# Expert weights in ten 16 KB places with 2 MB transfers, a front section laid out for them, and a filled router stretch

## The chip, the cores and the metric

The kernel runs on one core of a Trainium2 chip, as a single program. The metric is the device time of one execution in microseconds (us); lower is better. Before the change the median of three runs is 1062.04 us (1060.44 to 1062.28).

A core has a matrix engine (TensorE, PE in the profile, with its weight loads shown apart as PEld), a vector engine (VectorE, DVE), an activation engine (ScalarE, ACT), GpSimd (POOL) and a small engine that here only issues transfers (SyncE, SP). Sixteen DMA engines move data between the main memory and the on-chip memory SBUF, which has 128 partitions. TensorE accumulates in PSUM banks of 512 floats per partition. TensorE's clock has two levels, 1.2 and 2.4 GHz; the profile shows the granted one as a share of the full speed.

## The reference, cut to what matters

One encoder layer on 256 tokens of width 1024, in float32: token mixing by three mixers side by side, a LayerNorm, and then a mixture of 32 experts, of which each token uses 4, and a second LayerNorm.

```
z = x @ w_in + b_in                                   # 1024 -> 2304
y_pool = pool_mixer(z[0:256])                         # 4 centred means, a small linear map, a scale
y_attn = neighbourhood_attention(q, k, v, rpb)        # 8 heads of 64, tokens on a 4 x 64 grid, 16 columns wide
y_conv = conv_module(a, gate)                         # GLU, 31 taps, LayerNorm, swish, 256 x 256
x = layer_norm(ALPHA * x + concat(y_pool, y_attn, y_conv) @ w_out + b_out)
logits = x @ w_router + b_router
gates = softmax over the 4 largest logits, 0 elsewhere
for e in range(32):
    g = min(x @ w_gate[e] + b_gate[e], 7);  u = clip(x @ w_up[e] + b_up[e], -7, 7)
    out += gates[:, e] * (((u + 1) * g * sigmoid(1.702 * g)) @ w_down[e] + b_down[e])
x = layer_norm(ALPHA * x + out)
```

Each expert has three matrices of 1024 x 1024 floats, 12 MiB; all 32 are 384 MiB and have to pass through SBUF once. Everything else that is read is below 20 MiB.

## The kernel before

The program is written in order, engine by engine; nothing reorders it. It has two halves.

**The front.** The input projection is done in five column groups (`W_IN_GROUPS`): convolution, q, k, pooling, v. For q, k and v each raw weight is split into a high and a low part (`split`, lines 105 to 108: ACT makes the high part, DVE the rest), and three fast products stand for one exact one (`zstep`). Scores, softmax, the products with the values, the pooling and the 31 convolution taps (on DVE, in portions `TAPS`) follow, then the output projection `outproj`, whose weights come as four raw tiles of 1 MB (`wo_raw`). Three of them are split as well; the one in `WHOLE` is used as it is, by a full float32 product. Then come LayerNorm (`stats1`, `apply1`), the transposed activations `hT` (`turn1`), the router's scores, the choice of the four experts per token (`chosen`), and the slot of each token at its expert (`positions`). I call the time from the router's scores to the first expert product the router stretch: PE, DVE and ACT hand small results to each other there.

**The experts.** Each expert takes up to 64 tokens, gathered by a product with a 0/1 matrix (`gather`, line 729, out of `x1n`, which is `xa`). The products with the gate, up and down matrices are lines 761, 761 and 814 (`first`, `down`), each preceded by a product that puts the bias in (line 755). One matmul keeps 64 tokens as its stationary operand and streams 512 weight columns. The results are added to the four PSUM banks `acc` by line 826. The expert with the most tokens is put at number 20 (`FULL`) and gets a second, smaller block there.

**Weights.** SBUF holds twenty places of 8 KB per partition, 1 MiB each over 128 partitions (`slot`, line 89). A weight matrix comes as four transfers of 1 MiB, one per place (`load_rows`, line 136; the transfer itself is line 141), with a row of 8 KB for each partition. The places are taken in the order `places` (line 317) again and again. During the front many of these places hold the front's own tiles, and a weight transfer into such a place has to wait until the front is done with it. `load_ahead` issues expert 0's twelve transfers at three points of the front, and `load_expert` issues those of one further expert each time. All of them go out through SP, in program order: a transfer that waits for its place holds up everything behind it. Besides the place, each transfer waits until the eighth transfer before it has landed, since eight completion semaphores are used in turn.

**What sets the order around the change.** On SP it is the order of the calls; what a transfer waits for is the last reader of its place. On PE the router stretch runs: scores of tokens 128 to 255 (line 611), slots (635, 634, 635), the gather for expert 0 (729), the count of tokens per expert (1007), the bias of expert 0's gate (755) and its gate product (761).

The functions that the diff touches, as they were:

Of the kernel before, what the change touches and what calls it, by code (L numbers as in the profile page):

```python
# [25 lines left out]
CAP2 = 32  # L26
FULL = 20
# [19 lines left out]
def shape_consts():  # L47
# [3 lines left out]
    m = np.full((128, 2, 4, 31), -1e30, np.float32)  # L51
    for q in range(128):
        c2, i = q // 64, 15 - q % 16
        for pair in range(2):
            cb = 2 * pair + c2
            sc = min(max(cb * 16 + i - 8, 0), 48)
            for j in range(31):
                if sc <= BC[cb] + j < sc + 16:
                    m[q, pair, :, j] = 0.0
# [15 lines left out]
def encoder_layer(ctx, tc, xT_d, x_d, w_in, par_d, rows_d, rpb, w_out, cst_d,  # L75
# [14 lines left out]

    def bank(tag="bk"):
# [18 lines left out]
    def load_in(c0, n, places, h0=0):  # L110
# [3 lines left out]
        for h, place in enumerate(places, h0):  # L114
            t = slot(place, f"wi{place}")[:].rearrange("p (k c) -> p k c", c=n)
            nc.sync.dma_start(t, w_in_at[c0][:, h * per:(h + 1) * per, :])
            v.append(t)
        return v

    def halves(places, n):  # L120
        return [slot(p, f"wp{p}", F32R)[:].rearrange("p (k c) -> p k c", c=n) for p in places]

    class Parts:
# [5 lines left out]
        def add(self, raw, places, eng=nc.vector):  # L129
            self.v.append(halves(places, 2048 // self.per))  # L130
            split(raw, *self.v[-1], eng)
# [14 lines left out]
    xT = slot(0, "xT")[:].rearrange("p (k t) -> p k t", k=8)  # L146
    wi_conv = [slot(p, f"wi{p}")[:].rearrange("p (k c) -> p k c", c=512) for p in (1, 2)]
# [4 lines left out]
    wi_q = load_in(256, 512, (3, 4))  # L152
    nc.sync.dma_start(par[:], par_d)
    wi_k = load_in(768, 512, (13, 19))
    wi_p = load_in(0, 256, (14,))

    biasT = slot(17, "biasT")[:].rearrange("p (a h k) -> p a h k", a=2, h=8)
# [20 lines left out]
    wi_v = load_in(1280, 512, (1, 2))  # L178
# [39 lines left out]
    xh, xl = [slot(p, f"x{p}", F32R)[:].rearrange("p (k t) -> p k t", k=8) for p in (15, 16)]  # L218
# [38 lines left out]
    wp_q.add(wi_q[0], (9, 10))  # L257
    wp_q.add(wi_q[1], (11, 12))
    qbs = [bank("bg" if j == 3 else "bk") for j in range(4)]
    zproj(wp_q, qbs)  # L260
    wp_k.add(wi_k[0], (5, 6))
# [5 lines left out]
    wp_k.add(wi_k[1], (7, 8))  # L267
# [21 lines left out]
    wp_v.add(wi_v[0], (9, 10))  # L289
    wp_v.add(wi_v[1], (11, 12))  # L290
    run_taps(TAPS[5])
    add_mask(1)
    qk = slot(18, "qk")[:].rearrange("p (a c t) -> p a c t", a=2, c=4)
    qT, kT = qk[:, 0], qk[:, 1]
    for j in range(4):
        nc.scalar.activation(qT[:, j, :].rearrange("p (b r i) -> p r b i", b=4, r=4),
                             qbs[j][:, :256].rearrange("p (r b i) -> p r b i", r=4, b=4)[:, :, :, ::-1], AF.Identity,
                             bias=bias_in(2 + j), scale=1.0)
    zproj(wp_k, bks)
    for j in range(4):  # L300
        nc.scalar.activation(kT[:, j, :], bks[j][:, :256], AF.Identity, bias=bias_in(6 + j), scale=1.0)
    bias_parts()
    wo_raw = {k: load_rows(p, w_out, k) for k, p in ((1, 21), (0, 3), (2, 4), (3, 13))}
    xa = slot(19, "xa")[:].rearrange("p (t d) -> p t d", t=2)
    nc.sync.dma_start(xa, x_d.rearrange("p (t d) -> p t d", t=2))
    WHOLE = (0,)
    wo_places = ((5, 6), (7, 8), (1, 2), (9, 10))
    wo = {}

    def split_out(k):  # L310

        hi, lo = [slot(p, f"wo{p}", F32R)[:].rearrange("p (k c) -> p k c", k=2) for p in wo_places[k]]
        wo[k] = hi, lo
        assert k not in WHOLE
        split(wo_raw[k], hi, lo)
# [4 lines left out]
    chunks = ((m, k) for m in range(3) for k in ((0, 1, 2, 3), (0, 1, 2, 3), (0, 2, 1, 3))[m])  # L320
# [7 lines left out]

    act_table(AF.Exp)
# [5 lines left out]
    load_ahead(2)  # L335
# [895 lines left out]
```

## Time and profile before

| what | value |
|---|---|
| median of 3 runs | 1062.04 us (1060.44 to 1062.28) |
| profiled execution, its own time | 1060.73 us |
| its span, first to last instruction | 1058.9 us |
| granted TensorE clock, mean | 0.981 |
| PE busy | 986.5 us (93%) |
| DVE, ACT, POOL busy | 307.0, 161.7, 16.3 us |
| bytes moved by DMA | 423.38 MB, mean 400 GB/s |

The span is what the trace covers; the 1.8 us between it and the execution's own time lie around the program. PE's busy share is no measure of how near PE is to its peak. What counts is which wait ends last in each stretch, so the span has to be read in stretches: the front up to about 120 us, the experts after it, and the last 15 us, in which the last bytes have landed and the second LayerNorm and the stores follow. A DMA share near 1.00 means that all sixteen engines always have work.

### The profile page before, as it was taken

Reading aid. Unit: us, or ns where it says so; the run is one execution under the profiler, and the core shown is the slowest. Engines: PE = TensorE matmul, PEld = TensorE weight load, DVE = VectorE, ACT = ScalarE, POOL = GpSimd, SP = SyncE. Lnnn points to the kernel's source line nnn. Section 1 sums busy time; section 2 is a strip of 40 time slices with the busy share of each in tenths; the row PEclk is TensorE's granted clock in tenths of the full one; section 3 lists DMA queues with packets and bytes.
Section 4 is the critical chain, followed back from the end, with each engine's and each line's share of the span. In section 5 each row is a group of like instructions: output and inputs, shape, how many; then the busy total and the mean of one; then the engine's idle time right before and its main releaser. Section 6 shows DMA issues by size and latency. Waiting matters only on the chain.

```text
span 1058.9 us, 13693 instructions
## 1 busy us (share of the span) xinstructions
PE 986.5 (93%) x5202; PEld 431.9 (41%) x5202; DVE 307.0 (29%) x791; ACT 161.7 (15%) x339; POOL 16.3 (2%) x28
## 2 busy tenths in 40 slices
PE   7999999999999999999999898989999998998995
PEld 6977644343434343434333232333434332323232
DVE  4798442222212321212222112221222222112114
ACT  4374211011111011110101010110111110101001
POOL 0110000000000000000000000000000000000001
PEclk9999799999999899999999999999999999999998
DMA  9957799999999999999999999999999999999994
GB/s 373 402 213 318 274 377 421 421 422 421 420 421 421 420 421 421 421 421 421 421 422 418 422 421 421 420 423 419 421 421 422 420 421 421 422 421 420 421 397 169
DMA packets 61710, 423.38 MB, mean 400 GB/s; under 512 B 6886, under 2 KB 7398, under 8 KB 11594
## 3 DMA queue, kind: packets, MB, share of 16 engines
q1 hardware_dynamic: 61114, 421.82, 96.7%
q8 instruction: 42, 0.69, 0.3%
q0 software_dynamic: 384, 0.39, 0.1%
q10 hardware_dynamic: 144, 0.26, 0.1%
q14 instruction: 26, 0.21, 0.1%
HBM read 421.01 MB, written 1.05 MB: 399 GB/s over the span
## 4 chain that ended last, share of the span: by engine, by line
DMA 51%; PE 42%; DVE 3%; ACT 2%; issue 1%; SPq 0%; DVEq 0%; ACTq 0%
DMA w<-in_w_up_dram 18%; DMA w<-in_w_down_dram 16%; DMA w<-in_w_gate_dram 13%; PE bk L761 11%; PE bk L814 10%; PE bg L761 9%; PE bk L729 4%; PE acc L436 2%; DMA cst<-in_cst_dram 2%; DMA wi<-in_w_in_dram 2%; PE acc L826 1%; PE bk L791 1%; DVE cacc L277 1%; ACT sb L358 1%; PE bk L708 1%
## 5 line engine op out<-in xcount | busy, mean ns | idle before, releaser
L761 PE MATMUL bk<-w,xgp 128*64 128x512 f32 x1024 | 239.7, 605 | 13.1 <-DMA w<-in_w_up_dram 13.1
L761 PE MATMUL bg<-w,xgp 128*64 128x512 f32 x1024 | 233.8, 603 | 11.2 <-DMA w<-in_w_gate_dram 11.1
L814 PE MATMUL bk<-w,aT 128*64 128x512 f32 (+1 forms) x1024 | 227.0, 600 | 1.5 <-DMA w<-in_w_down_dram 1.5
L761 PEld LDWEIGHTS bg<-w,xgp 128*64 128x64 f32 x1024 | 72.5, 139 | 161.7 <-issue 118.9
L761 PEld LDWEIGHTS bk<-w,xgp 128*64 128x64 f32 x1024 | 69.1, 138 | 151.6 <-issue 108.3
L814 PEld LDWEIGHTS bk<-w,aT 128*64 128x64 f32 (+1 forms) x1024 | 69.7, 137 | 136.2 <-issue 127.5
L819 DVE SCALAR_TENSOR_TENSOR y<-bk,gs,y 128x512 fp32r<-128x512 f32 x31 | 23.3, 751 | 270.1 <-ACT y L818 270.1
L770 DVE TENSOR_SCALAR g<-bg 128x512 f32<-128x512 f32 x32 | 22.1, 692 | 172.8 <-PE bg L761 172.8
L729 PE MATMUL bk<-se,xa 128*128 128x128 f32 (+1 forms) x544 | 66.8, 284 | 0.5 <-DVE se L720 0.5
L729 PEld LDWEIGHTS bk<-se,xa 128*128 128x128 f32 x544 | 65.3, 200 | 0.6 <-issue 0.6
L793 ACT COPY aT<-bk 128x256 f32<-128x256 f32 (+1 forms) x66 | 24.3, 369 | 240.7 <-PE bk L791 236.2
L771 ACT ACTIVATE s<-g 128x512 f32<-128x512 f32 (+1 forms) x33 | 20.6, 625 | 250.7 <-DVE g L770 250.7
L781 DVE TENSOR_SCALAR u<-bk 128x256 f32<-128x256 f32 (+1 forms) x66 | 27.5, 417 | 93.6 <-PE bk L761 93.6
L818 ACT ACTIVATE y<-bk,gs 128x512 fp32r<-128x512 f32 x31 | 21.3, 687 | 215.2 <-PE bk L814 215.2
L826 PE MATMUL acc<-y,st 64*128 64x512 f32 x248 | 46.3, 447 | 1.1 <-ACT y L818 0.8
L791 PE MATMUL bk<-ident,g 128*128 128x128 f32 x128 | 27.6, 298 | 13.6 <-DVE g L782 12.4
L577 DVE TENSOR_SCALAR xgp<-bk,g1b 128x128 f32<-128x128 f32 (+1 forms) x68 | 22.7, 397 | 51.6 <-PE bk L729 51.6
L575 ACT ACTIVATE xgp<-bk,g1b 128x128 f32<-128x128 f32 (+1 forms) x68 | 25.1, 450 | 82.0 <-PE bk L729 82.0
L711 DVE TENSOR_SCALAR st<-bk 128x256 fp32r<-128x256 f32 x32 | 13.6, 425 | 82.3 <-PE bk L708 82.3
L826 PEld LDWEIGHTS acc<-y,st 64*128 64x128 f32 x248 | 19.1, 186 | 32.0 <-issue 29.5
L772 DVE TENSOR_TENSOR g<-g,s 128x512 f32<-128x512 f32 (+1 forms) x33 | 22.6, 684 | 24.6 <-ACT s L771 24.6
L791 PEld LDWEIGHTS bk<-ident,g 128*128 128x128 f32 x128 | 13.3, 143 | 37.5 <-issue 22.4
(289 smaller groups left out, 666.3 us busy)
## 6 DMA issues: line engine op xcount, KB each, us to landing
w<-in_w_gate_dram SPq DMA_DIRECT2D x127, 1024.0 KB, 19.8
w<-in_w_up_dram SPq DMA_DIRECT2D x127, 1024.0 KB, 19.8
w<-in_w_down_dram SPq DMA_DIRECT2D x124, 1024.0 KB, 19.8
wi<-in_w_in_dram SPq DMA_DIRECT2D x8, 1024.0 KB, 9.8
w<-in_w_out_dram SPq DMA_DIRECT2D x4, 1024.0 KB, 9.3
w<-in_w_down_dram SPq DMA_DIRECT2D x7, 512.0 KB, 8.7
wi<-in_w_in_dram SPq DMA_DIRECT2D x2, 512.0 KB, 6.9
biasT<-in_rpb_dram SPq DMA_DIRECT2D x2, 512.0 KB, 17.5
```

The source lines that it names most:

```text
L575: nc.scalar.activation(o, i, AF.Identity, bias=b, scale=g)
L577: eng.tensor_scalar(o, i, g, b, op0=mult, op1=add)
L729: nc.tensor.matmul(p[:, i * n:(i + 1) * n], x1n[:, tt, (g + i) * 128:(g + i) * 128 + 128], se[:, tt, :], start=(tt == 0), stop=(tt == 1))
L761: nc.tensor.matmul(p[i * c:(i + 1) * c, :n], xg[:, k, :], w[k // 2][:, k % 2, i * n:(i + 1) * n], start=False, stop=(k == 7))
L770: nc.vector.tensor_scalar(g[:], p[:, :n], 7.0, None, op0=ALU.min)
L772: nc.vector.tensor_tensor(g[:], g[:], s[:], op=mult)
L781: nc.vector.tensor_scalar(u[:, o], p[:, o], -7.0, 7.0, op0=ALU.max, op1=ALU.min)
L791: nc.tensor.transpose(p[:, j * 128:j * 128 + 128], a[:, j * 128:j * 128 + 128], ident[:])
L793: nc.scalar.copy(aT[:, o], p[:, :h * 256].rearrange("p (j n) -> p j n", n=128)[:, o])
L814: nc.tensor.matmul(p[o:o + c, :], aT[:, k % h, k // h * c:(k // h + 1) * c], rows_of(w, k, dh), start=(k == of_part[0]), stop=(k == of_par ...
L819: nc.vector.scalar_tensor_tensor(y[:, 1], p[:], gs[:], y[:, 0].bitcast(F32), op0=mult, op1=sub)
L826: nc.tensor.matmul(acc[tt][dh][:], st[dh * 64:dh * 64 + 64, tt, :], y[dh * 64:dh * 64 + 64, i, :], start=(start and i == 0), stop=False, s ...
```

## The change

1. **Places and transfers.** The twenty places of 8 KB become ten of 16 KB (`both`). An expert matrix comes as two transfers of 2 MiB, with a row of 16 KB per partition; `by_chunks` lays the arrays out for that on the host. The rows of the down matrix are stored in the order in which `down` uses them (`DOWN`).
2. **Front.** The front's tiles are put into halves of the new places, in other neighbourhoods, with two places of 8 KB beside them (19 and 20). Expert 0's transfers are issued at four points of the front, and the tile `xa` and the raw output weights 0 and 3 are loaded later.
3. **Expert 1's down matrix** is loaded back into the tiles of expert 0's gate matrix, in five pieces, so that a piece can start as soon as the rows that it overwrites have been used.
4. **Keys and values by grid column.** `kT` and the new `vT` are written with the four tokens of a grid column side by side, so that the 31 columns that a block needs are 124 neighbouring floats. The sixteen copies for `vB` become four. The rpb bands and the mask are laid out to match.
5. **Output projection.** Raw tile 3 is used whole, like tile 0; its split and the low parts for rows 6 and 7 go.
6. **Router stretch.** The sums of the router weights are reduced on DVE first (`gsum`), and one matmul of 64 columns takes the place of eight. Behind the first slots, PE gets the bias product of expert 0's gate (`p0`) and a product of `hT` with the identity into an `acc` bank, which nothing reads. The count of tokens per expert moves ahead of the gather. The gather for expert 1 moves from the middle of expert 0's up product to its transposes, in two halves.

Where the transfers stand on SP: this is the piece of SP's queue before from the raw output weights (`in_w_out_dram`) to the first load of the table `whose`, which tells which expert comes when; a row is one kind of transfer with its count.

```order
L141 DMA w<-in_w_out_dram 128x2048 x4
L305 DMA xa<-in_x_dram 128x2048
L141 DMA w<-in_w_gate_dram 128x2048 x4
L141 DMA w<-in_w_up_dram 128x2048 x4
L141 DMA w<-in_w_down_dram 128x2048 x4
L141 DMA w<-in_w_gate_dram 128x2048 x4
L141 DMA w<-in_w_up_dram 128x2048 x4
L141 DMA w<-in_w_down_dram 128x2048 x4
L928 TENSOR_LOAD whose
```

And the same piece of SP's queue now; `xT`, `wo` and `bias` are the tiles whose halves hold raw output weights.

```order
L143 DMA xT<-in_w_out_dram 128x2048
L143 DMA wo_439<-in_w_out_dram 128x2048
L150 DMA w<-in_w_gate_dram 128x4096 x2
L150 DMA w<-in_w_up_dram 128x4096
L143 DMA wo_447<-in_w_out_dram 128x2048
L150 DMA w<-in_w_up_dram 128x4096
L143 DMA bias<-in_w_out_dram 128x2048
L150 DMA w<-in_w_down_dram 128x4096 x2
L515 DMA xa<-in_x_dram 128x2048
L150 DMA w<-in_w_gate_dram 128x4096 x2
L150 DMA w<-in_w_up_dram 128x4096 x2
L150 DMA w<-in_w_down_dram 128x1024 x2
```

Six weight transfers of 2 MiB now stand between and ahead of the last raw output weights and `xa`; expert 1's down matrix starts with two pieces of 0.5 MiB (three of 1 MiB follow), where it was four transfers of 1 MiB.

PE's queue in the router stretch before, from the second half of the router's scores to the gate product of expert 0 (`bk` and `bg` are PSUM banks, `msk` the chosen experts, `se` the 0/1 matrix of the gather):

```order
L611 MATMUL bk<-gw,hT 128x32 x8
L635 MATMUL bk<-msk,cst 128x32
L634 MATMUL bk<-msk,onesm 128x32
L635 MATMUL bk<-msk,cst 128x32
L729 MATMUL bk<-se,xa 128x64 x16
L1007 MATMUL bk<-msk,onesm 128x32 x2
L755 LDWEIGHTS bsel
L755 MATMUL bg<-bg_101,bsel 64x512
L761 MATMUL bg<-w,xgp 64x512 x16
```

The same stretch of PE's queue now:

```order
L631 MATMUL bk<-gw,hT 128x32 x8
L655 MATMUL bk<-msk,cst 128x32
L678 LDWEIGHTS bsel
L678 MATMUL bg<-bg_98,bsel 64x512
L704 MATMUL acc_72<-hT,ident 128x512
L654 MATMUL bk<-msk,onesm 128x32
L655 MATMUL bk<-msk,cst 128x32
L671 MATMUL bk<-msk,onesm 128x32 x2
L767 MATMUL bk<-se,xa 128x64 x16
L806 MATMUL bg<-w,xgp 64x512 x16
```

The bias and the identity product stand between the first and the second slots, the count stands ahead of the gather, and the gate product follows the gather directly.

The core of the diff:

```diff
+    def both(i, name, dtype=F32):
+        t = slots.tile([128, 4096], dtype, name=name, tag=f"p{i}")[:]
+        return t, (t[:, :2048], t[:, 2048:])
...
-    def load_rows(place, src, k, n=1):
-        t = slot(place, "w")[:]
-        for i in range(n):
-            o = slice(i * 2048 // n, (i + 1) * 2048 // n)
-            nc.sync.dma_start(t[:, o], src[k][:, o])
-        return t.rearrange("p (k c) -> p k c", k=2)
+    def load_rows(place, src, k, cuts=(0, 4), t=None):
+        t = both(place, "w")[0] if t is None else t
+        for a, b in zip(cuts, cuts[1:]):
+            nc.sync.dma_start(t[:, a * 1024:b * 1024], src[k][:, a * 1024:b * 1024])
+        return t.rearrange("p (k c) -> p k c", k=4)
...
-    wo_raw = {k: load_rows(p, w_out, k) for k, p in ((1, 21), (0, 3), (2, 4), (3, 13))}
-    WHOLE = (0,)
-    wo_places = ((5, 6), (7, 8), (1, 2), (9, 10))
+    wo_raw = {1: load_out(wo1, 1), 2: load_out(both(6, "wo2")[1][0], 2)}
+    WHOLE = (0, 3)
+    wo_places = {1: 8, 2: 5}
...
-    places = (5, 6, 0, 15, 16, 21, 4, 11, 12, 3, 13, 7, 8, 1, 2, 18, 14, 9, 10, 17)
+    places = (0, 1, 2, 3, 7, 4, 8, 5, 6, 9)
...
+    load_ahead(3)
+    wo_raw[0] = load_out(slot(19, "wo0")[:], 0)
...
-    vB = slot(17, "vB")[:, :1984].rearrange("p (j b k) -> p j b k", j=4, b=4)
+    vT = b_v[:, :1024].rearrange("p (j t) -> p j t", j=4)
...
-    b = bank()
-    for k in range(8):
-        nc.tensor.matmul(b[:, :64], onesm[:], gw[:, k], start=(k == 0), stop=(k == 7))
+    nc.vector.tensor_reduce(gsum[:], gw[:].rearrange("p k e -> p e k"), axis=AX.X, op=add)
...
+    b = bank()
+    nc.tensor.matmul(b[:, :64], onesm[:], gsum[:], start=True, stop=True)
...
     positions(0)
+    p0 = bank("bg")
+    bias_first(p0, bsel[:, 0:1], 0)
+    nc.tensor.matmul(acc[0][0][:], ident[:], hT[:, 0:2, :], start=True, stop=True)
     chosen(1, i1)
     positions(1)
+    call = keep.tile([128, E], F32, name="call")
+    counts()
...
-        p = first(sel, 0, xg, W[0], tag="bg")
+        p = first(sel, 0, xg, W[0], tag="bg", p=p0 if e == 0 else None)
+        if e == 0:
+            first_tiles = [W[0][k].rearrange("p k c -> p (k c)") for k in range(2)]
+            Wn[2] = {k: load_rows(next(turns), w_down[1], k, ((0, 1, 2, 4), (0, 2, 4))[k], first_tiles[k])
+                     for k in range(2)}
...
-def by_chunks(w):
-    return w.reshape(*w.shape[:-2], 4, 2, 128, 1024).swapaxes(-3, -2).reshape(*w.shape[:-2], 4, 128, 2048)
+def by_chunks(w, n=2, order=range(8)):
+    w = w.reshape(*w.shape[:-2], 8, 128, 1024)[..., list(order), :, :]
+    return w.reshape(*w.shape[:-3], n, 8 // n, 128, 1024).swapaxes(-3, -2).reshape(*w.shape[:-3], n, 128, 8192 // n)
```

## Rows read from the trace of the kernel before

**Rows 1.** The page, bandwidth in 40 equal slices of the span.
```profile
GB/s 373 402 213 318 274 377 421 421 422 421 420 421 421 420 421 421 421 421 421 421 422 418 422 421 421 420 423 419 421 421 422 420 421 421 422 421 420 421 397 169
```

**Rows 2.** The page, the chain of work that ended last, by engine.
```profile
DMA 51%; PE 42%; DVE 3%; ACT 2%; issue 1%; SPq 0%; DVEq 0%; ACTq 0%
```

**Rows 3.** Stretches: stretch and length, busy per engine, PEclk, DMA share, GB/s.
```profile
40.00:120.00 80.00, 75.48 (x546) 64.13 (x545) 65.51 (x141) 41.33 (x102) 9.32 (x17) 0.96 0.78 305
120.00:130.00 10.00, 10.00 (x37) 4.26 (x39) 5.39 (x33) 2.13 (x4) 0.00 (x0) 0.63 0.35 118
130.00:160.00 30.00, 28.55 (x154) 12.06 (x152) 13.48 (x62) 3.35 (x8) 0.00 (x0) 1.00 0.97 380
160.00:1020.00 860.00, 812.41 (x4138) 309.74 (x4136) 189.60 (x501) 94.92 (x205) 0.00 (x0) 0.99 1.01 421
```

**Rows 4.** Timeline of PE: starts of three experts, and the first waits for weights.
```profile
518.04 0.39 PE L755 MATMUL bg<-bg,bselp 96*64 96x512 bf16 x2
542.27 0.39 PE L755 MATMUL bg<-bg,bselp 96*64 96x512 bf16 x2
570.08 0.39 PE L755 MATMUL bg<-bg,bselp 96*64 96x512 bf16 x2
593.01 1.94 PE L814 MATMUL bk<-w,aT 128*64 128x512 f32 x8 [0.25 <-DMA w<-in_w_down_dram]
```

**Rows 5.** What SP waited for: total us, times, longest us.
```profile
SPq L141 <- PE bg L761: 32.2, 22, 14.2
```

**Rows 6.** Timeline of SP's transfer issues: start us, us, then what.
```profile
106.58 4.99 SPq L141 DMA_DIRECT2D w<-in_w_up_dram  x4
125.89 6.36 SPq L141 DMA_DIRECT2D w<-in_w_down_dram  x4
```

**Rows 7.** Timeline of PE, router stretch and first experts: start us, us, then what.
```profile
113.06 0.41 PE L635 MATMUL bk<-msk,cst 128*128 128x32 f32 x2 [1.44 <-DVE msk L628]
114.00 7.06 PE L729 MATMUL bk<-se,xa 128*128 128x64 f32 x32 [0.54 <-DVE se L720]
120.86 1.01 PE L1007 MATMUL bk<-msk,onesm 128*128 128x32 f32 x4
122.22 9.65 PE L761 MATMUL bg<-w,xgp 128*64 128x512 f32 x32
...
135.74 3.68 PE L729 MATMUL bk<-se,xa 128*128 128x64 f32 x32
...
152.62 7.04 PE L761 MATMUL bg<-w,xgp 128*64 128x512 f32 x32
```

**Rows 8.** The page: a transfer queue (packets, MB, share), issues (KB, us to landing).
```profile
q8 instruction: 42, 0.69, 0.3%
...
w<-in_w_gate_dram SPq DMA_DIRECT2D x127, 1024.0 KB, 19.8
...
w<-in_w_down_dram SPq DMA_DIRECT2D x7, 512.0 KB, 8.7
```

**Rows 9.** A stretch in which the last expert's 512 KB transfers land.
```profile
1038.00:1040.00 2.00, 2.00 (x12) 0.72 (x10) 0.00 (x0) 0.06 (x1) 0.00 (x0) 1.00 1.05 387
```

**Rows 10.** Timeline of PE, output projection and the sums for the router.
```profile
73.85 3.70 PE L436 MATMUL acc<-w,more 128*128 128x512 f32 x8 [2.16 <-ACT more L411]
...
79.49 3.70 PE L436 MATMUL acc<-w,more 128*128 128x512 f32 x8
...
90.41 5.85 PE L436 MATMUL acc<-wo,mix 128*128 128x512 f32 x24
96.09 1.90 PE L529 MATMUL bk<-gw,onesm 128*128 128x64 f32 x16
...
99.48 4.62 PE L436 MATMUL acc<-wo,mix 128*128 128x512 f32 x18
...
104.73 1.62 PE L436 MATMUL acc<-wo,mix 128*128 128x512 f32 x6
```

**Rows 11.** Timeline of DVE: the first use of the tile xa.
```profile
94.44 2.49 DVE L522 SCALAR_TENSOR_TENSOR xa<-xa,small 128x512 f32<-128x512 f32 x4
```

More of the change, by code (lines that the diff above doesn't have):

```diff
@@ L26 @@
 CAP2 = 32
+DOWN = (0, 1, 4, 5, 2, 3, 6, 7)
 FULL = 20
@@ L127, in __init__, with add @@
             self.per, self.v = 2048 // n, []
-        def add(self, raw, places, eng=nc.vector):
-            self.v.append(halves(places, 2048 // self.per))
+        def add(self, raw, place, eng=nc.vector):
+            self.v.append(halves(place, "wp", 2048 // self.per))
             split(raw, *self.v[-1], eng)
@@ L382, in encoder_layer @@
             zstep(bks[j], wp_v, k, j)
[L384 to L389 removed]
+    load_ahead(1)
+    wo_raw[3] = load_out(k_wo, 3)
     nc.vector.reciprocal(rs[:], sm[:])
@@ L645, in gates, with counts, bias_first @@
         nc.vector.tensor_scalar(gat[:, tt], gat[:, tt], nm[:, 1:2], None, op0=mult)
+    def counts():
+        b = bank()
+        for tt in range(2):
+            nc.tensor.matmul(b[:, :32], onesm[:], msk[:, tt], start=(tt == 0), stop=(tt == 1))
+        nc.vector.tensor_copy(call[:], b[:, :32])
+    def bias_first(p, sel, m, c=CAP):
+        n = 8 * c
+        for i in range(128 // c):
+            nc.tensor.matmul(p[i * c:(i + 1) * c, :n], sel.to_broadcast([96, c]),
+                             bg3[:96, m, i * n:(i + 1) * n], start=True, stop=False)
     stats1(0, 0)
@@ L748, in gather_few, with first @@
                 affine((nc.scalar, nc.vector)[j % 2], xg[:, i * h + j, :], p[:, i * c:(i + 1) * c], i * h + j)
-    def first(sel, m, xg, w, c=CAP, tag="bk", between=(8, None)):
-        p = bank(tag)
+    def first(sel, m, xg, w, c=CAP, tag="bk", between=(8, None), p=None):
         n = 8 * c
-        for i in range(128 // c):
-            nc.tensor.matmul(p[i * c:(i + 1) * c, :n], sel.to_broadcast([96, c]),
-                             bg3[:96, m, i * n:(i + 1) * n], start=True, stop=False)
+        if p is None:
+            p = bank(tag)
+            bias_first(p, sel, m, c)
         for k in range(8):
@@ L938, in load_expert @@
             return v + [load_last(of_place(w_down)), brow2]
-        return v + [{k: load_rows(next(turns), of_place(w_down), k) for k in (0, 2, 1, 3)}]
+        return v + [load(w_down) if e > 1 else None]
     def further():
@@ L980, in late @@
     def late():
-        spare = itertools.cycle([next(turns) for _ in range(len(places) - 14)])
+        spare = itertools.cycle([next(turns) for _ in range(len(places) - 7)])
         jobs = nc.values_load(many[0:1, 0:1], min_val=0, max_val=JOBS)
@@ L999, in late @@
                 scatter(stx[0], down(turn(ax, "x"), dict(enumerate(Wx[2])), stx[1], "x"))
-    load_ahead(5)
-    def counts():
-        b = bank()
-        for tt in range(2):
-            nc.tensor.matmul(b[:, :32], onesm[:], msk[:, tt], start=(tt == 0), stop=(tt == 1))
-        nc.vector.tensor_copy(call[:], b[:, :32])
+    load_ahead(3)
     def places_of():
```

200 lines of the change are left out of this document (104 added, 96 removed).

## The prediction

> **What bounds the kernel now.** I read the bandwidth over time first. From the seventh slice on it stands at 418 to 423 GB/s to the last but one [rows 1]; the loss lies in the first six slices and in the last two. The stretches say the same: 421 GB/s at a DMA share of 1.01 from 160 to 1020 us, and less ahead of that [rows 3]. Next comes the chain, which is misread easily: it gives DMA 51% and PE 42% [rows 2], as if a faster PE were worth something. The timeline of PE corrects that. Two experts in a row take 570.08 - 518.04 = 52.0 us of PE, 26.0 each, if nothing waits [rows 4]. The stream needs 12 MiB, 12.58 MB, at 421 GB/s, 29.9 us. PE starts with twenty full places and eats that lead up; the first wait for weights after the start stands at 593 us [rows 4]. Up to there the chain runs through PE, and yet the end is set by DMA: the stream never stops, and PE ends a fixed tail after it.
>
> So the time is: when the weight stream gets under way without gaps, plus the bytes left then over the rate, plus a tail. Work saved on PE, DVE or ACT counts only where it moves the first or changes the second.
>
> When does it get under way? By 120 us the twenty places are full: the 40 to 120 stretch moves at 305 GB/s, that is 80 x (1 - 305/421) = 22 us without transfers, but what these gaps cost is only that the places fill at 120 and not earlier. Then SP waits for a place 14.2 us at once, for expert 0's gate product [rows 5], from 111.6 (106.58 + 4.99) to 125.89 [rows 6]. From 120 to 130 DMA moves 118 GB/s [rows 3], a gap of 10 x (1 - 118/421) = 7.2 us. PE is late there since its clock is down: 0.63 on average from 120 to 130 [rows 3]. The gather takes 7.06 us, while the same 32 instructions take 3.68 for expert 1, and the gate product takes 9.65 against 7.04 [rows 7].
>
> **Restart of the stream.** The first transfer that needs a place from expert 0 is now a piece of 0.5 MiB that overwrites one row block of the gate weights, the first of eight, so it waits for 4 of the 32 matmul instructions, not for 8. Where does the gate product start? The gather started at 114.00 [rows 7]. Ahead of it stands the count now (1.01 us at half clock [rows 7], so 0.5 at full, and a copy on DVE that the slots wait behind): +0.6. In the output projection 24 instructions of 4.62 + 1.62 = 6.2 us become 16 of the full kind, at 3.70/8 each 7.4 us: +1.2; the router sums go from 16 instructions of 1.90 us to 2, -1.7 [rows 10]. Small hand-overs with DVE pace that stretch too, so I bound the two by -0.5 and +0.5 and take +0.3, since the longer products stand last. The gather then starts at 114.9. The bias product is already done, so the gate product follows directly.
>
> At full clock: 114.9 + 3.68 = 118.6, and 4/32 of 7.04 is 0.9, so SP is released at 119.5 in place of 125.89: 6.4 us gained. At half clock, as before: 114.9 + 7.06 = 122.0, and twice 0.9, so 123.7: 2.2 us gained. Which one depends on whether the clock keeps up. In the stretch before it fell, PE did little but products of 32 columns; now it gets the bias product and two instructions of 512 columns (0.46 us each by rows 10) there. That is more, but only some 1.5 us, and the gather with its 64 columns comes after it. I take the middle, 4.5 us gained. What the sequence of frees does from there on: from 130 to 160 the stream lost 30 x (1 - 380/421) = 2.9 us [rows 3]. With places of 2 MiB I expect one dry spell of about 2 us when expert 0's down product frees its first place, because gather work for expert 1 now stands ahead of that product. I put the difference at 0, with 2.9 us on either side.
>
> This needs the ten places to be full by then. Two of the last three go free with the output products of channels 512 to 767, at 96.3 (90.41 + 5.85); two transfers of 2 MiB, 5.0 us each, land by 108. The last one holds raw output weight 3 and goes free with the last output product, about 106.5 (104.73 + 1.62, a little later for the longer products) [rows 10]. So it is full at about 113, against a restart at 119.5 or later: 6 us of slack. That slack is what hides the front's edits. Fewer copies for the values, contiguous keys and one split less cost or bring nothing, unless they move the gather. The tile `xa` is issued later now, behind expert 0's last transfer, after the second pair of output products (79.49 + 3.70 = 83.2 [rows 10]); behind that transfer's 5 us it lands near 89, and DVE needs it at 94.44 [rows 11]: 5 us of cover, and beyond that each microsecond would move the router stretch.
>
> **Rows of 16 KB.** Each engine handles rows one by one. At 421 GB/s, 26.3 GB/s per engine, a row of 8 KB takes 311.3 ns. The profile has rows of 2 KB too: the last expert's down transfers of 512 KB [rows 8], and their best stretch runs at 387 GB/s [rows 9], 84.7 ns a row. Two points make a line: 226.6 ns for 6144 bytes more, 36.9 ns per KB and 9.2 ns fixed per row. A row of 16 KB then takes 9.2 + 604.3 = 613.5 ns, 427.3 GB/s, 1.5% more. That is an estimate from two stretches. Bounds: no gain if a row is cut into 8 KB again, and a loss if long rows run worse (below). That packets of 16 KB exist shows in the instruction queue: 42 packets, 0.69 MB [rows 8], though they share engines with the stream and give no clean price.
>
> At the restart 20 of 384 MiB are in. Of the 364 left, 4 MiB are the pieces of expert 1's down matrix, 4 MiB the last down matrix and 4 MiB the cut transfers of expert 31, all with shorter rows. 352 MiB, 369.1 MB, take 876.7 us at 421 and 863.8 at 427.3: 12.9 us gained. PE can follow: it needs 26.0 us per expert, the stream would need 29.4.
>
> The Trainium skill, page "DMA: Bandwidth & Descriptors", section "Where 436 GB/s comes from", puts the ceiling of the SBUF side at 435.2 GB/s. No run here shows it; by it the same 369.1 MB would take 848.1 us, a gain of 28.6 us, if nothing fixed were left per row.
>
> **The tail.** The last expert's down matrix keeps its rows of 2 KB and its pieces of 512 KB. I put the tail at 0.
>
> **Sum.** The profiled execution took 1060.73 us, 1.3 under the median of 1062.04. 1060.7 - 4.5 - 12.9 = 1043.3. I predict 1043; a median of new runs may lie a microsecond above that.
>
> **Rivals.**
> (a) Rows of 16 KB are no faster; only the restart is left. For it: the line rests on a stretch in which PE and SP also paced the transfers. Against: those would make 2 KB rows look slow, and 387 is the best of them. Time: 1060.7 - 4.5 = 1056.2, and 1058.5 with the clock down.
> (b) The rate goes to the ceiling, with the fixed part of a row gone altogether: 1060.7 - 4.5 - 28.6 = 1027.6. Against it: the fixed part belongs to each row, and only half of the rows go.
> (c) Ten places are too coarse. After the restart PE frees 2 MiB each 26.0/6 = 4.3 us and the stream takes 5.0, so the cushion grows by only 0.6 us per transfer, and a gather or a turn between two products eats it. If the first six transfers each end with a gap of 1.3 us (what lies between the issue at 125.89 and the end of the gap at 127.2), 8 us are lost: 1051. Against it: before, with half the grain, the loss was 2.9 us in all.
> (d) Slower: long rows run worse in the main memory. Each row is then a run of twice the length, at twice the distance from the next, and the sixteen engines may get into each other's way. It decides from 876.7 us x 0.5%: below 418.9 GB/s in the stream the restart's 4.5 us are eaten. If the rate falls by as much as I expect it to rise, the time is 1060.7 - 4.5 + 12.9 = 1069.1. For it: nothing in the profile shows a stream of such rows. Against it: from 2 to 8 KB the stream gained with the length [rows 3, 9].
> The same page, section "Latency and other measured facts", lists copies that lose from 3% up to half at row distances of 512 KiB and more, and none at smaller ones; here the distance goes from 8 to 16 KiB, and no run shows that case.
>
> **Chances.** Forecast as said, with the clock up or down: 0.62 (own range 1037 to 1048). (a) 0.17, (b) 0.05, (c) 0.08, (d) 0.08. The range that should hold 8 in 10 is 1036 to 1057: it takes in the forecast, (c) and most of (a), and leaves out (b), (d) and the end of (a). Below 0.2%, 2.1 us, this kernel's runs can't be told apart. Faster than that: 0.62 + 0.05 + most of (a) and (c), 0.89; within it 0.04, from (a) with the clock down and (c); slower 0.07, from (d).
>
> **What would show it.** In the changed profile: GB/s per stretch near 427 from 160 to 1020 (421 speaks for (a), 418 or less for (d)); SP's longest wait for the gate product ending near 119.5 to 124; the granted clock between 110 and 130, and the gather at 3.7 or 7.1 us; the ten places full near 113; gaps in DMA between 125 and 200 us beyond 3 us speak for (c). The prediction is wrong if PE waits for weights again right after the start, if `xa` lands after 94 us, or if the tail behind the last landing grows.

## The result, and the profile after

The changed kernel takes 1043.88 us, the median of four runs; the kernel before took 1062.16 beside it. The ratio is 0.9837 (95% interval 0.9812 to 0.9861). The four runs are not spread around the median: two took 1040.36 and 1041.09 us at a mean clock of 0.989, two took 1046.67 and 1046.97 at 0.981 and 0.983. The profiled execution is the one of 1040.36 us (span 1038.5), 20.4 us under the profiled execution of before.

Bandwidth in 40 slices after, against [rows 1]:

```profile
GB/s 373 384 331 300 273 422 426 425 428 426 426 428 427 426 427 426 427 428 427 427 425 426 430 425 428 426 425 425 428 426 427 426 426 427 426 427 427 425 401 174
```

From the seventh slice on it stands at 425 to 430 where it stood at 418 to 423. The mean of those 32 slices is 426.5; of before it is 420.9. The sixth slice, in which the experts begin, has gone from 377 to 422.

The stretches after, against [rows 3] (busy time of PE, PEld, DVE, ACT, POOL, then PEclk, DMA share, GB/s):

```profile
0.00:160.00 160.00, 150.84 (x974) 110.53 (x976) 104.98 (x272) 62.31 (x119) 10.42 (x21) 1.00 0.89 349
...
40.00:120.00 80.00, 76.57 (x545) 60.56 (x546) 65.31 (x150) 38.52 (x89) 10.23 (x17) 1.00 0.81 309
120.00:130.00 10.00, 10.00 (x50) 3.38 (x48) 5.49 (x27) 2.76 (x5) 0.00 (x0) 1.00 0.95 339
130.00:160.00 30.00, 30.00 (x176) 14.76 (x172) 14.17 (x65) 4.76 (x12) 0.00 (x0) 1.00 1.01 422
```

And one stretch of the kernel before that was not shown, the first 160 us in one piece:

```profile
0.00:160.00 160.00, 148.27 (x940) 112.17 (x942) 104.22 (x267) 63.02 (x127) 9.52 (x21) 0.96 0.83 327
```

These rows give the balance. By 160 us the changed kernel has moved (349 - 327) x 160 = 3.5 MB more, 8.4 us of the stream at 421: 5.2 us of it between 120 and 130, 3.0 between 130 and 160. The other 367.5 MB take 873.1 us at 420.9 GB/s and 861.7 at 426.5: 11.4 us. The sum is 19.8 of the 20.4 us; a rate rounded by 0.5 GB/s is worth 1 us.

SP's issues after, against [rows 6] (start, duration, then what):

```profile
96.61 9.87 SPq L150 DMA_DIRECT2D w<-in_w_up_dram  x2
119.02 6.34 SPq L150 DMA_DIRECT2D w<-in_w_down_dram  x5
128.68 4.29 SPq L150 DMA_DIRECT2D w<-in_w_gate_dram  x2
140.33 3.77 SPq L150 DMA_DIRECT2D w<-in_w_up_dram  x2
```

PE in the router stretch after, against [rows 7]:

```profile
111.43 1.12 PE L704 MATMUL acc<-hT,ident 128*128 128x512 f32 x2
...
114.21 3.75 PE L767 MATMUL bk<-se,xa 128*128 128x64 f32 x32 [0.54 <-DVE se L759]
117.90 7.09 PE L806 MATMUL bg<-w,xgp 128*64 128x512 f32 x32
```

In this execution the clock did not fall: the gather takes 3.75 us in place of 7.06, the gate product follows it at once, and SP is released at 119.02 in place of 125.89.

### The profile page after: what moved, and what is told of

Same layout as the page of the kernel before. It is cut to its first block, busy times and chain, and to the rows that moved or that the text cites. A ratio compares the mean times of both kernels' runs of the same rounds, so it can differ in the third digit from the quotient of the medians.

```text
span 1038.5 us, 12916 instructions
## 1 busy us (share of the span) xinstructions
PE 971.7 (94%) x5182; PEld 428.7 (41%) x5182; DVE 304.8 (29%) x789; ACT 158.9 (15%) x326; POOL 17.3 (2%) x28
## 4 chain that ended last, share of the span: by engine, by line
PE 60%; DMA 33%; DVE 4%; ACT 1%; issue 1%; DVEq 0%; POOL 0%; SPq 0%; ACTq 0%
DMA w<-in_w_up_dram 18%; PE bk L806 15%; PE bk L852 14%; PE bg L806 13%; DMA w<-in_w_down_dram 8%; DMA w<-in_w_gate_dram 8%; PE bk L767 4%; PE acc L864 2%; PE acc L263 2%; PE bk L836 2%; PE acc L452 1%; DVE cacc L292 1%; PE acc L237 1%; PE acc L238 1%; PE acc L239 1%; PE bk L747 1%
## 5 line engine op out<-in xcount | busy, mean ns | idle before, releaser
L806 PE MATMUL bk<-w,xgp 128*64 128x512 f32 x1024 | 234.2, 600 | 15.0 <-DMA w<-in_w_up_dram 15.0
L806 PE MATMUL bg<-w,xgp 128*64 128x512 f32 x1024 | 228.6, 597 | 7.9 <-DMA w<-in_w_gate_dram 7.9
L767 PE MATMUL bk<-se,xa 128*128 128x128 f32 (+1 forms) x528 | 61.7, 275 | 0.5 <-DVE se L759 0.5
L767 PEld LDWEIGHTS bk<-se,xa 128*128 128x128 f32 x528 | 60.3, 192 | 0.6 <-issue 0.6
L836 PE MATMUL bk<-ident,g 128*128 128x128 f32 x128 | 27.5, 297 | 11.9 <-DVE g L827 11.4
L827 DVE SCALAR_TENSOR_TENSOR g<-u,g 128x256 f32<-128x256 f32 x64 | 27.2, 425 | 2.2
```

Of the source, the lines that this page charges most:

```text
L767: nc.tensor.matmul(p[:, i * n:(i + 1) * n], x1n[:, tt, (g + i) * 128:(g + i) * 128 + 128], se[:, tt, :], start=(tt == 0), stop=(tt == 1))
L806: nc.tensor.matmul(p[i * c:(i + 1) * c, :n], xg[:, k, :], w[k // 4][:, k % 4, i * n:(i + 1) * n], start=False, stop=(k == 7))
L827: nc.vector.scalar_tensor_tensor(a[:, o], u[:, o], 1.0, g[:, o], op0=add, op1=mult)
L836: nc.tensor.transpose(p[:, j * 128:j * 128 + 128], a[:, j * 128:j * 128 + 128], ident[:])
```

## The experiments

Theory A: the gain is the length of a row (the rate) plus the restart of the stream; how much of the restart comes depends on whether TensorE keeps its full clock, 2.4 GHz, through the router stretch or drops to 1.2. The rivals give the gain to the size of a transfer, to the larger places or to the new front, or take the two levels for noise. Experiments 1 to 4, 5 to 8 and 9 to 12 each ran beside the kernel before, each group on another chip, with medians of 1061.35, 1060.33 and 1060.15 us for that kernel. So a difference of about 1 us between groups is not safe.

### 1 and 2: rows of 8 KB in the changed kernel

`e1_rows8` cuts the row and leaves the transfer at 2 MiB; `e2_cut1m` cuts both.

```diff
 # e1_rows8 (arrays laid out in four row blocks instead of two)
-nc.sync.dma_start(t[:, a * 1024:b * 1024], src[k][:, a * 1024:b * 1024])
+nc.sync.dma_start(t.rearrange("p (h c) -> p h c", h=2), src[2 * k:2 * k + 2].rearrange("h p c -> p h c"))
 # e2_cut1m
-def load_rows(place, src, k, cuts=(0, 4), t=None):
+def load_rows(place, src, k, cuts=(0, 2, 4), t=None):
```

> The changed kernel with each 2 MiB weight transfer left whole, but laid out in main memory as two halves, so that it consists of 256 rows of 8 KB in place of 128 rows of 16 KB; places, order, waits and everything else unchanged. Theory A (the length of a row sets the rate): the stream falls from 426 back to 421 GB/s, 369.1 MB take 10 to 13 us more, so about 1054 to 1057 us against 1043.9. Theory B (the size or number of transfers sets the rate, or the larger places do): the rate stays at 426 and the time at 1040 to 1047.

> The changed kernel with each whole 2 MiB weight transfer issued as two of 1 MiB into the same place, each with 128 rows of 8 KB. Theory A (row length): as with rows of 8 KB in one transfer, 421 GB/s and 1054 to 1057 us; twice the number of issues costs nothing, since SyncE waits for places anyway. Theory B (transfer size): slower here by the same 10 us, while the 2 MiB transfers of 8 KB rows lose nothing. If both runs stay at 1040 to 1047, the gain in rate has another source.

Measured: 1059.1 us (1055.31 to 1061.03, 11 runs; ratio to before 0.9976, 0.9965 to 0.9987) and 1055.73 (1054.95 to 1061.65, 10 runs; 0.9972, 0.9954 to 0.9990). The second median is as expected; the first lies above the 1054 to 1057 expected. The stretch from 160 to 1000 us of both:

```profile
160.00:1000.00 840.00, 785.90 (x4040) 304.96 (x4040) 185.34 (x492) 92.92 (x201) 0.00 (x0) 0.99 1.01 420
```

```profile
160.00:1000.00 840.00, 791.33 (x4026) 299.34 (x4022) 184.11 (x489) 91.33 (x197) 0.00 (x0) 0.99 1.01 419
```

The changed kernel has 426 there. Transfers of 2 MiB with rows of 8 KB are as slow as those of 1 MiB, so it is the row and not the transfer. The six fastest runs of `e2_cut1m`, 1054.95 to 1056.05 at a clock of 0.986 to 0.990, lie 14 to 15 us above the changed kernel's lower level: a little more than the 10 to 13 expected, since the rate fell to 419 and not 421. The profiled run of `e1_rows8` is one with the clock down (0.77 on average from 120 to 130 us): over the first 160 us it moves 335 GB/s where `e2_cut1m` moves 348, 5.0 us of the stream, and that is what lies between its 1061.03 us and the 1056.05 of the other profile. How many of its other runs are of that kind no profile shows.

### 3 and 4: the filler taken out, and two more put in

```diff
 # e3_no_filler
-nc.tensor.matmul(acc[0][0][:], ident[:], hT[:, 0:2, :], start=True, stop=True)
 # e4_three_fillers (behind the first one, and behind counts())
+nc.tensor.matmul(acc[0][1][:], ident[:], hT[:, 2:4, :], start=True, stop=True)
+nc.tensor.matmul(acc[1][0][:], ident[:], hT[:, 4:6, :], start=True, stop=True)
```

> The changed kernel without the product of the identity with hT in the router stretch, whose result is never read; the early bias product of expert 0 and the count ahead of the gather stay. Theory A (the runs of the changed kernel at 1046.7 and 1047.0 us are those in which TensorE's clock fell to half in the router stretch, those at 1040.4 and 1041.1 the ones in which it did not): without that product the clock stands at 0.50 through the gather in every run, the gather takes 7 us in place of 3.75, SyncE is released near 124 in place of 119.0, and every run takes 1046 to 1048 us with a mean clock of 0.981 to 0.983. Rival (the two levels have another cause, and the early bias product alone keeps the clock up): times spread from 1040 to 1047 as before, or all lie near 1040.

> The changed kernel with two more such products, whose results are never read: one directly behind the first, one between the count and the gather. By the profile each takes 1.1 us of TensorE, of which about 0.6 to 1.6 us in all stand ahead of the gather. Theory A: the clock stays at 1.00 through the gather in every run; all runs within 1 us of each other, at 1040 to 1043 us with a mean clock of 0.989. Rival (the two levels have another cause): times still fall into two groups 5 to 6 us apart, each 1 to 2 us later than those of the changed kernel.

Without the filler all four runs took 1046.21 to 1047.79 us at 0.983 (ratio to before 0.9874, 0.9860 to 0.9888). The gather of that kernel:

```profile
114.57 6.93 PE L766 MATMUL bk<-se,xa 128*128 128x64 f32 x32 [0.54 <-DVE se L758]
```

```profile
123.45 7.17 SPq L150 DMA_DIRECT2D w<-in_w_down_dram  x5
```

The gather runs at half clock and SP is released at 123.45, as expected. With three fillers the five runs took 1041.91 to 1044.29 us: the level near 1047 did not come, but two runs, 1043.6 and 1044.3 at 0.986, lie between the levels, which theory A did not foresee ("within 1 us" missed).

### 5 and 6: a filler in the wait ahead of the gather, and the changed kernel again

```diff
 # e5_gap_filler
-    counts()
+    counted = counts()          # without its copy
+    nc.tensor.matmul(acc[1][0][:, :256], ident[:], hT[:, 4, :], start=True, stop=True)
...
+    se = slots_of([of(posm, 0)])
+    nc.vector.tensor_copy(call[:], counted[:, :32])
```

> The changed kernel with a second product of the identity, of 256 columns (result never read), in the 0.54 us in which TensorE waits between the count and the gather; and VectorE copies the count behind the two slot instructions, not ahead of them. Theory A (the clock in the router stretch decides between the two levels): the gather starts 0 to 0.3 us earlier than at 114.21, the clock holds at 1.00 through it in all or nearly all runs, and the median is 1040 to 1042 us, below the changed kernel and below the version with two long extra products. Rival (the second product does nothing for the clock): two groups of times 6 us apart, as often as in the changed kernel.

> The changed kernel as it is, to see how often each of the two levels comes on the same chip as the next runs. Theory A: every run lies either at 1040 to 1042 us with a mean clock of 0.989 or at 1046 to 1048 with 0.981 to 0.983, nothing between. Rival (the spread is noise of the chip): the runs spread over the whole stretch, and so do those of the version with the second filler.

The changed kernel again: 1046.3 us at 0.983 (profiled), and 1044.52, 1044.57, 1044.88 at 0.986. So there is a third level, and "nothing between" was wrong. With the second filler: 1040.17, 1040.33 and 1040.65 us, but also 1046.95 and 1047.19. Its lower level is the lowest of the kernels here, yet it does not come in every run: the median of 1040.65 was as expected, "nearly all runs" was not. The profiled run of it is a late one:

```profile
111.77 2.07 PE L704 MATMUL acc<-hT,ident 128*128 128x512 f32 x2
...
116.19 6.93 PE L768 MATMUL bk<-se,xa 128*128 128x64 f32 x32
```

The first filler itself takes 2.07 us in place of 1.12: here the clock fell at 111.7, and the second filler stands at 115.20. In this run what decided lies ahead of it. On this chip 7 of 10 runs with the second filler (numbers 5 and 8) kept to the lower level and none of the four of the changed kernel, of which two of four had kept to it in the first set; so the second filler may help, but these counts do not show it.

### 7: the kernel before with the router stretch alone changed

```diff
     positions(0)
+    p0 = bank("bg")
+    bias_first(p0, bsel[:, 0:1], 0)
+    nc.tensor.matmul(acc[0][0][:], ident[:], xa[:, 0, :512], start=True, stop=True)
     chosen(1, i1)
     positions(1)
+    counts()
```

> The kernel before, with its twenty 8 KB places, 1 MiB transfers, front and order, and only the router stretch changed: expert 0's gate bias product and one product of the identity (512 columns of xa, result never read) behind the first positions, and the count ahead of the gather. Theory A (the gain is the rate of 16 KB rows plus the restart, the front's new layout brings nothing): where the clock holds, the gather takes 3.7 us in place of 7.06, SyncE is released at 119 to 121 in place of 125.89, and the time is 1054 to 1057 us, the same as the changed kernel with rows of 8 KB at the full clock (1055); where it falls, 1059 to 1062. Rival (the front's new layout or the larger places carry part of the gain): 1058 to 1061 even where the clock holds.

Measured: 1057.91 us (1056.38 to 1062.94, 11 runs; ratio 0.9988, 0.9973 to 1.0002, so no gain clear of noise), its profiled run 1057.18 with the clock up, between what theory A and what the rival expected:

```profile
119.66 5.48 SPq L141 DMA_DIRECT2D w<-in_w_down_dram  x4
```

```profile
130.00:160.00 30.00, 28.55 (x161) 13.49 (x160) 12.79 (x60) 4.87 (x12) 0.00 (x0) 1.00 0.98 398
160.00:1000.00 840.00, 790.78 (x4026) 298.88 (x4026) 185.42 (x492) 91.42 (x197) 0.00 (x0) 0.99 1.01 419
```

SP is released 6.2 us earlier than before, and over the first 160 us this run moves 345 GB/s where before it was 327, 6.8 us of the stream; yet it is only 3.6 us faster than the profiled one of before. Its stream ran at 419 where the same transfers ran at 421 in the profile of before, which takes 4 us back; the 2.8 us that remain are the 3.6 within the rounding of the rates. Against the changed kernel it also loses from 130 to 160 (398 GB/s for 422, 1.7 us), which number 10 explains. All four profiles with 8 KB rows have one constant rate each, 419, 419, 420 and 421; what sets it within these 2 GB/s no run here shows. Runs of this kernel at the same mean clock of 0.987 took 1056.93 and 1060.71 us, so with these rows the mean clock alone does not tell the time.

### 8: whole transfers for expert 1's down matrix

```diff
-Wn[2] = {k: load_rows(next(turns), w_down[1], k, ((0, 1, 2, 4), (0, 2, 4))[k], first_tiles[k])
+Wn[2] = {k: load_rows(next(turns), w_down[1], k, (0, 4), first_tiles[k])
```

> The kernel with the second filler, and expert 1's down matrix loaded into expert 0's gate places in two whole transfers of 2 MiB in place of five pieces, so that SyncE waits for half of the gate product (16 of 32 matmul instructions) and not for 4 of them. Theory A (the end moves by as much as the restart of the stream): SyncE is released 12 instructions of 0.22 us later, at 121.6 in place of 119.0, and the time grows by 2.0 to 3.0 us over the version with the pieces. Rival (the stream catches up, since TensorE has twenty MiB in hand): the same time within 0.5 us.

Measured: 1040.83, 1041.3, 1041.69 (profiled, with the clock up) and 1041.97 us, and one of 1047.17. Against the three lower runs of `e5_gap_filler` the four lower ones are 1.1 us more, between the two expectations. SP's release is 2.2 us later than in the changed kernel's profile:

```profile
121.20 3.76 SPq L150 DMA_DIRECT2D w<-in_w_down_dram  x2
```

```profile
140.00:150.00 10.00, 10.00 (x50) 3.33 (x48) 3.94 (x15) 0.69 (x1) 0.00 (x0) 1.00 1.01 427
```

The changed kernel has 397 in that stretch:

```profile
140.00:150.00 10.00, 10.00 (x50) 3.35 (x48) 4.33 (x18) 0.69 (x1) 0.00 (x0) 1.00 0.98 397
```

With pieces the stream is early and runs dry once more when expert 0's down product frees its first place at 140.3; with whole transfers SP waits for that place too, until 139.9, but earlier transfers are then still under way. By the bytes the pieces bring little. They start 2.2 us earlier, but from the release to 130 us the stream loses 2.9 us with pieces (339 GB/s from 120 to 130) and 1.4 with whole transfers (310), and 0.4 us more from 130 to 160 (422 against 427). Over the first 160 us the two kernels move 349 and 348 GB/s, 0.4 us of the stream apart. So most of the earlier restart is given back; where the rest of the 1.1 us in the times comes from no run shows.

### 9: rows of 4 KB

The edit is that of `e1_rows8` with eight row blocks, on top of the second filler.

> The kernel with the second filler, with its 2 MiB transfers laid out as 512 rows of 4 KB. Theory A (each row costs 36.9 ns per 1000 bytes and 9.2 to 9.6 ns beside): 160 to 161 ns a row, 407 to 409 GB/s, and for the 367 MB behind 160 us some 37 us more than with rows of 16 KB: 1077 to 1084 us. Rival (the fixed part of a row is not what separates 8 from 16 KB; only the step to 16 KB helps): the rate stays at 419 to 421 GB/s, 1054 to 1062 us.

Measured: 1080.26 us (1079.26 to 1084.34, 4 runs; ratio to before 1.0198, 1.0170 to 1.0225), at

```profile
160.00:1000.00 840.00, 767.87 (x3930) 295.72 (x3928) 180.48 (x481) 90.01 (x195) 0.00 (x0) 0.99 1.02 409
```

409 GB/s is 160.2 ns a row; the line of the prediction gives 36.9 x 4.096 + 9.2 = 160.3. The line held at a row length between the two from which it was drawn, 2 and 8 KB.

### 10: expert 1's gather back in the middle of the up product

```diff
             if e == 0:
                 got.append(select(sg))
+                sg1 = pick(of(pos1, 1), of(gate1, 1))
+                gather(se, xgp[:, 0, :, CAP:], CAP)
+                got.append(select(sg1))
```

> The kernel with the second filler, with expert 1's gather put back into the middle of expert 0's up product, where the kernel before had it; its selection moves with it. Theory A (the order of frees decides between 130 and 160 us): the second up place is free near 136 in place of 132.5, the stream runs dry for about 2 us there, and the gap of 1.1 us ahead of expert 0's first down place goes; the net is a loss of 0.5 to 2 us against the version with the second filler at the same clock, and 405 to 420 GB/s from 130 to 160 us in place of 422 to 427. Rival (the late gather brings nothing): 422 GB/s or more there and no difference.

Measured: 1041.76 (profiled, with the clock up), 1042.01 and 1042.17 us, and one of 1048.38; the first three are 1.6 us above the lower runs of `e5_gap_filler`. The stretch, SP's issues into the two up places, and PE behind the up product:

```profile
130.00:160.00 30.00, 28.55 (x159) 13.26 (x160) 12.91 (x60) 4.87 (x12) 0.00 (x0) 1.00 0.98 397
```

```profile
128.04 8.04 SPq L150 DMA_DIRECT2D w<-in_w_gate_dram  x2
```

```profile
136.68 0.44 PE L837 MATMUL bk<-ident,g 128*128 128x128 f32 x2 [0.98 <-DVE g L828]
```

397 GB/s, as the kernel before with the router edits has (398): with the gather in the old place the new front and the coarse places lose just what the old ones lost. SP has issued into the second up place at 136.1 (128.04 + 8.04), in the changed kernel at 133.0 (128.68 + 4.29). PE idles here too, ahead of the transposes for the down product: 28.55 of 30 us busy in both, 30.00 in the changed kernel. This run and that of `e7_old_router_edits` have moved the same by 160 us (346 and 345 GB/s), and of the 15.4 us between 1041.76 and 1057.18 the rate, 426 against 419, makes 367.5 MB x 0.0392 us per MB = 14.4.

### 11 and 12: wider products earlier in the router stretch

```diff
-nc.tensor.matmul(b[:, :32], hT[:, k, tt * 128:tt * 128 + 128], gw[:, k, :32], ...)
+n = 128 if k < 7 else 64
+nc.tensor.matmul(b[:, :n], hT[:, k, tt * 128:tt * 128 + 128], gw[:, k:k + n // 64], ...)
```

> The kernel with the second filler, in which the sixteen score products of the router move 128 columns each (the last of each row block 64) in place of 32; the columns beyond 32 are never read. By the neighbouring transposes of 128 columns (0.13 us each against 0.12) that costs 0.1 to 0.3 us ahead of the gather. Theory A (what TensorE does in the router stretch decides whether its clock stays up): all runs at 1040 to 1042 us with a mean clock of 0.987 or more. Rival (the level is drawn by chance and does not depend on this work): one to three runs in five lie at 1044 to 1048.

> The changed kernel without any product of the identity, whose score products move 128 columns as in the run before this one (columns beyond 32 never read). Without fillers and with 32 columns all four runs lay at 1046.2 to 1047.8. Theory A (columns moved keep the clock up, wherever in the stretch they stand): most runs at 1040 to 1042 us. Rival (only work in the wait just ahead of the gather helps): all runs at 1046 to 1048.

With wide scores and both fillers all five runs took 1040.65 to 1042.46 us, median 1041.34, at 0.988 to 0.991 (ratio to before 0.9819, 0.9800 to 0.9839). Its level is about 1 us above the three lower runs of `e5_gap_filler`, but none of its runs left it, and of all versions its interval lies lowest, though it overlaps with others. That it always holds is not shown: of the 18 runs of the four kernels with the same two fillers and narrow scores (numbers 5, 8, 9 and 10) 13 kept to their lower level, and five in a row would come by chance in about one case in five. Without fillers the four runs took 1044.96 to 1045.86 us at 0.983 to 0.986: neither expectation. The clock fell there as well, but later:

```profile
114.59 5.05 PE L768 MATMUL bk<-se,xa 128*128 128x64 f32 x32 [0.54 <-DVE se L760]
119.57 9.08 PE L807 MATMUL bg<-w,xgp 128*64 128x512 f32 x32
```

```profile
114.00:116.00 2.00, 1.46 (x14) 1.45 (x13) 0.52 (x3) 0.00 (x0) 0.00 (x0) 1.00 0.14 53
116.00:118.00 2.00, 2.00 (x15) 2.00 (x14) 0.00 (x0) 1.29 (x4) 0.00 (x0) 0.70 0.00 0
122.00:124.00 2.00, 2.00 (x8) 0.62 (x6) 1.44 (x13) 0.32 (x1) 0.00 (x0) 0.60 0.60 180
```

PEclk is 1.00 up to 116, 0.70 from 116 to 118 and 0.60 from 122 to 124: half speed from about 116.8 to 123.6. In the changed kernel's run of 1046.3 us it was from 111.4 to 125.0, by the first and the last of these rows:

```profile
111.00:112.00 1.00, 1.00 (x4) 0.62 (x3) 0.90 (x7) 0.78 (x2) 0.00 (x0) 0.70 0.96 393
114.00:116.00 2.00, 1.46 (x8) 1.36 (x8) 0.52 (x3) 0.00 (x0) 0.00 (x0) 0.50 0.01 4
...
124.00:126.00 2.00, 2.00 (x8) 0.52 (x6) 1.44 (x13) 0.32 (x1) 0.00 (x0) 0.74 0.56 162
```

So a time between the levels goes with a clock that falls only in the middle of the gather, which then takes 5.05 us; SP was released at 121.58. In `e3_no_filler` the clock fell at 114.7, just behind the start of the gather (0.68 on average from 114 to 116 us), the gather took 6.93, and the time is that of the early falls. The changed kernel's runs at 1044.5 to 1044.9 may be of the late kind; their mean clock, 0.986, is the same as here, but a run of `e8_whole_transfers` at 0.986 took 1041.97 us, and none of these three was profiled.

## Why the prediction was right, step by step

**Rows of 16 KB: right, a little less than worked out.** 426.5 GB/s for the 427.3 of the line (whose KB is 1000 bytes), 614.6 ns a row for 613.5, and 11.4 us for 12.9 [rows 3, 9]. The 1.5 us between are the 0.8 GB/s. Experiments 1, 2 and 9 put the whole of it on the row. Taken to rows without end, the line's 36.9 ns per 1000 bytes give 433.6 GB/s from sixteen engines, an estimate. The Trainium skill, page "DMA: Bandwidth & Descriptors", section "Where 436 GB/s comes from", puts the SBUF side at 435.2; the four row lengths agree with that and show how far each stays below: 387, 409, 419 to 421 and 426.5 GB/s. Rivals (a), (b) and (d) fall with the measured rate.

**Restart: right in its place and at the full clock; the middle between the clocks was the wrong value to take.** The gather started at 114.21 (114.9 predicted), the gate product at 117.90 (118.6), SP was released at 119.02 (119.5). The prediction took 4.5 us as the middle of full and half clock; the middle of its 6.4 and 2.2 is 4.3. Neither profile of the changed kernel shows the middle: SP is released at 119.02 with the clock up and at 123.77 with the clock down. A release in the middle, 4.3 us ahead of before, came in `e12_wide_no_fillers`, where the clock fell late. The times of the changed kernel come in groups, 1040 to 1041, 1044.5 to 1045 and 1046 to 1047 us. The median of 1043.88 agrees with 1043 only because two of four runs lay on either side: that is luck. Half clock was put at 4.2 us over full; by the release it was 123.45 - 119.02 = 4.4, and in the time some 6. Over the first 160 us `e3_no_filler` moves 334 GB/s and the changed kernel with the clock up 349, 5.7 us of the stream: 4.9 of it between 120 and 130 us, where PE runs at half clock up to 125, and 0.9 from 130 to 160 (410 against 422), where the places come free later.

**130 to 160: put at 0, was 3.0 us of gain.** This is the term that was mis-sized; 2.9 us was its stated bound [rows 3]. The prediction saw the gather for expert 1 ahead of the down product and expected a dry spell there. The dry spell is there but small (397 GB/s from 140 to 150, 0.7 us). What it did not see is that this gather left the middle of the up product, so that the second up place comes free sooner (133.0 for 136.1), and that it now fills the 1.45 us that PE waited ahead of the transposes before:

```profile
144.22 0.44 PE L791 MATMUL bk<-ident,g 128*128 128x128 f32 x2 [0.99 <-DVE g L782]
145.12 0.44 PE L791 MATMUL bk<-ident,g 128*128 128x128 f32 x2 [0.46 <-DVE tplace L1029]
```

Experiment 10 shows it: with the gather back in its old place, 397 GB/s. Rival (c), six gaps of 1.3 us, falls.

**Ten places full near 113, `xa` in time, front at 0: right.** The last two transfers before the restart are issued by 106.5 (96.61 + 9.87), DMA has fallen to 37 GB/s by 114 to 116, and SP waits until 119. DVE takes `xa` at 94.39 without a wait, against [rows 11]. That the new front, the coarse places and the pieces bring nothing in sum follows from experiments 7 and 10: the same bytes by 160 us. What each of them brings alone was not tried, but for the pieces (number 8).

**Tail 0: right.** The last two slices read 401 and 174 against 397 and 169.

The forecast of 17.4 us against the profiled execution's own time was 20.4 in that run: 1.5 less on the rate, 3.9 more on the start, and 0.6 left in rounding. The 3.9 are 2.4 at the release, where the clock stayed up, and 3.0 from 130 to 160, less 1.6 right behind the release, 3.8 in all: there the stream, taking its pieces one by one, moved 3.4 MB in the 11.0 us up to 130 and so lost 2.9 us, where before it moved 1.2 MB in 4.1 and lost 1.3.

## What to carry over

Where a kernel is bound by a stream of weights, work out what one row costs from two row lengths that the trace already has; the fixed part, here 9 ns a row, tells what longer rows bring. That larger transfers of the same rows bring nothing took runs of their own to show (numbers 1 and 2). A restart that hangs on a short chain of small products has a price for each level of TensorE's clock, and others if the clock falls within the chain; work out both ends and look at several runs, since one profile shows one of them. What an earlier restart gains can be lost again right behind it and at the next place that is freed late (2.2 us earlier was 0.4 us of bytes in number 8), so follow the frees until the stream has no gap.

## What the runs showed that was not expected

- The same program falls into levels of its own: the changed kernel's runs took 1040.4, 1041.1, 1046.7 and 1047.0 us in the first set and 1044.5, 1044.6, 1044.9 and 1046.3 in the second. In the profiles the clock fell at 111.4 in one run and not at all in this stretch in another, with the same instructions ahead of it to within 0.5 us. On which chip the first set ran is not known, so how far the levels go with the chip is open; both sets hold more than one.
- PE's busy time does not tell which. In the changed kernel it is busy for 8.76 of the 9 us from 100 to 109 and for all of 109 to 112, in the run in which the clock fell at 111.4 as in the one in which it did not fall. Just ahead of the fall in `e5_gap_filler` it is busy all the time:

```profile
110.00:111.00 1.00, 1.00 (x11) 1.00 (x11) 0.19 (x2) 1.00 (x2) 0.00 (x0) 1.00 1.15 459
111.00:112.00 1.00, 1.00 (x8) 0.73 (x8) 0.61 (x3) 1.00 (x3) 0.00 (x0) 0.87 0.94 377
```

  In `e11_wide_scores`, which has the same products in this stretch but for wider scores, the clock stays up:

```profile
110.00:111.00 1.00, 1.00 (x11) 1.00 (x11) 0.27 (x2) 1.00 (x2) 0.00 (x0) 1.00 0.97 360
111.00:112.00 1.00, 1.00 (x9) 0.73 (x9) 0.50 (x3) 1.00 (x3) 0.00 (x0) 1.00 1.02 410
```

- The sixteen score products take 1.97 us with 32 columns and 2.00 us with 128:

```profile
109.31 1.97 PE L631 MATMUL bk<-gw,hT 128*128 128x32 f32 x16 [0.24 <-ACT hT L623]
```

```profile
109.39 2.00 PE L632 MATMUL bk<-gw,hT 128*128 128x128 f32 x16 [0.24 <-ACT hT L623]
```

  The first row is of `e5_gap_filler`, the second of `e11_wide_scores`: the wider product cost next to nothing.
- The Trainium skill, page "TensorE: Matmul & The Clock Gate", section "Part 1: The HAM clock gate (the "warmup" mystery)", says that the slow clock is the default and that recent activity of the engine lifts it. That agrees with experiments 3, 4, 11 and 12 in direction; it does not explain the falls at 111.4 and 111.7, with PE busy all the time since 110, and why equal programs differ from run to run no run here shows.
